# Experts' further tokens in a routed MoE: the loop's work rearranged, and x times its norm gathered in place of the modulated x

## The chip, the cores and the metric

The kernel runs on one core of one Trainium2 chip. The metric is the device time of one execution in microseconds (us). Before: 2464.49 us, the median of 3 runs (2462.65 to 2467.65).

## What is computed

A network with one sequence of 256 tokens, width 1024, in fp32: first two layers that each have an attention mixer and a routed mixture of experts (MoE), then two layers of another block. The change touches the two MoE alone. With `x` the residual stream:

```python
h = rmsnorm(x, norm_ffn[layer]) * (1.0 + scale_f) + shift_f
x = x + gate_f * grouped_moe(h, ...)

# grouped_moe: 16 experts in 4 groups, 2 experts of one group a token
aff = sigmoid(xf @ router_w)
biased = (aff + router_b).reshape(T, N_GROUPS, EXPERTS_PER_GROUP)
grp_score = sum(top_k(biased, 2)[0], axis=-1)
g_sel = argmax(grp_score, axis=-1)
local = top_k(biased[tok, g_sel], 2)[1]
w = aff[tok, expert] / sum(aff[tok, expert])
# every token of every one of its two experts
hid = silu(xb @ w_gate[e]) * (xb @ w_up[e])
out[token] += w * (hid @ w_down[e])
```

How many tokens an expert gets is known only when the kernel runs. The weights of a layer's experts are 96 MB, read once.

## The kernel before

A scheduler orders the instructions of the whole program for each engine by priority and dependence; the code's order is its starting point. Weights come by SyncE's (SP's) queue into a ring of 12 slots of 1 MB, "w" (`SLOTS`, `CAP`, L861); `load` (L890) takes the next slot and issues the transfer, `fill` (L928) asks for as many tiles ahead as `cap` allows, `take` hands them out in order. fp32 matmuls leave two records each in the trace; those of fp32r operands (a rounded high part and its rest, "h" and "l") leave one.

`router_prep` (L1104) runs ahead of a MoE, beside the mixer: it transposes `mod[4]`, which holds scale times gain, and `mod[3]`, the shift, and multiplies the router's weights with them.

`moe_body` (L1895), once a layer:
- transposes x, multiplies it with the router's weights, and makes `rs`, the inverse norm of each token (L1916). On DVE: logits z (L1927), sigmoid on ACT (L1928), the biased bz (L1931), the choice of group and experts in some 15 small operations, up to `selb` (L1957); on PE the position of each token within its expert; on DVE `OH` (L1976), a one-hot of expert slots, 64 a expert.
- for each of two halves of 128 tokens: h = x rs mod[4] on DVE (L1984), + mod[3] on POOL (L1985), its rounded part `hTh` on ACT (L1988) and the rest `hTl` on DVE (L1989). The last two read h with a step of 8 elements and write contiguously, so that a block of 128 columns is a contiguous stationary operand.
- `gather(b)`, four times, four experts each: 32 matmuls (L2020) with a 128x128 block of hTh or hTl stationary and 256 columns of OH moving give `xT`, the experts' tokens by columns; ACT copies it out of PSUM, 128x256 at a time (L2024).
- eight pairs q of experts: `gateup(q)` takes 8 tiles (L2048), silu and product follow, `down(q)` takes 4 tiles (L2066), `combine` scatters with the transposed one-hot and adds to x (L2086, L2088), one pair late.
- an expert's tokens beyond 64 go through `overflow` (L2126), called at q = 5 (`QL`). It is a loop whose number of passes is read at run time, one for each further 64 tokens of an expert: none in layer 0 of this input, one in layer 1.

A pass finds the expert on DVE (L2173 to L2178), reads its number into SP (L2179), and issues six transfers into six slots `lw` (L2183, L2186): gate and up, two tiles each, and down, two. The down product of a pass is `tail()` (L2150 to L2166): it is called within a pass for the pass before, and once behind the loop for the last one. Where there is no pass before, it multiplies zeros: POOL clears `hk`, `wk`, `ohT` and two whole `lw` tiles first (L2136). Between, the pass gathers its tokens (L2205 to L2218) and does gate and up (L2225 to L2231). Ahead of the loop `fill` asks for six tiles of q = 5 (`CAPL`).

```python
n = nc.values_load(nw[0:1, 0:1], min_val=0, max_val=7)
with s.tc.For_i(0, n, 1):
    ...
    ei = nc.sync.value_load(nw[0:1, 1:2], min_val=0, max_val=15)
    ...
    tail()
```

Of the kernel before, what the change touches and what calls it, by code (L numbers as in the profile page):

```python
# [57 lines left out]
class Kern:  # L58
# [781 lines left out]
class Full(Kern):  # L840
# [20 lines left out]
    SLOTS, CAP, SPL, DEEP, CAPL = 12, 11, 3, 7, 6  # L861
# [87 lines left out]
    def setup1(s):  # L949
# [15 lines left out]
        s.rlb = B1.tile([128, 16], F32, name="rlb")  # L965
        s.onesb = B1.tile([128, 128], BF, name="onesb")
# [3 lines left out]
        s.late.append(lambda: nc.sync.dma_start(s.rwp, I["router_w"].rearrange("(k p) e -> p k e", p=128)))  # L970
# [134 lines left out]
    def router_prep(s):  # L1105

        nc, V = s.nc, s.nc.vector
        for j in range(2):
            p = s.trans4(s.mod[4][:, j * 512:(j + 1) * 512])
            V.tensor_tensor(s.rwg[:, 4 * j:4 * j + 4, 0:16], s.rwp[:, 4 * j:4 * j + 4], p[:, :, 0:16], op=OP.mult)  # L1110
            yield
        q = s.bank("bg", (128, 16))
        for j in range(2):
            p = s.trans4(s.mod[3][:, j * 512:(j + 1) * 512])
            sh = s.a2("sh")
            nc.scalar.copy(sh, p)
            for k in range(4):
# [757 lines left out]
    def moe_srcs(s, l):  # L1875
        g, u, d = (s.I[n][l] for n in ("moe_w_gate", "moe_w_up", "moe_w_down"))
        out = []
        for m, j in s.FILL[l]:
            out += s.ada_src(m, j)
        for e in range(0, 16, 2):  # L1880
            for w in (g, u):
                for h in range(2):
                    for i in range(2):
                        out.append((w[e + i].rearrange("(p k) n -> p k n", p=128)[:, 4 * h:4 * h + 4], True))
            for h in range(2):
                for i in range(2):
                    out.append((d[e + i].rearrange("(p k) n -> p k n", p=128)[:, 2 * h:2 * h + 2], True))
        return out
# [6 lines left out]
    def moe_body(s, l, end):  # L1895
# [26 lines left out]
        nc.scalar.copy(lg, p)  # L1922
        p = s.bank("bg", (128, 2, 16))
# [33 lines left out]
        V.tensor_copy(selb, sel)  # L1957
# [20 lines left out]

        hh = []
        for t in range(2):  # L1980
            h = hb[t]
            hi = s.hp.tile([128, D], F32R, name=f"hTh{t}")
            lo = s.hp.tile([128, D], F32R, name=f"hTl{t}")
# [6 lines left out]
            hh.append((hi, lo))  # L1990
# [20 lines left out]
        def gather(b):  # L2011
            for i in range(2):
                xT[2 * b + i] = A.tile([128, 8, 128], F32, name="xT", tag="xT", bufs=3)
            for c in range(0, 8, 2):
                p = s.bg()
                for cc in range(2):
                    first = True
                    for t in range(2):
                        for x in hh[t]:
                            nc.tensor.matmul(p[:, cc * 256:(cc + 1) * 256], x[:, (c + cc) * 128:(c + cc + 1) * 128], OH[t][:, 4 * b:4 * b + 4],  # L2020
                                             start=first, stop=t == 1 and x is hh[t][1])
# [70 lines left out]
        for q in range(8):  # L2092
            if q == s.QL - 1:
                s.cap = s.CAPL
            if q == s.QL:
# [3 lines left out]
                tail = s.overflow(l, hh, pos, W, nx, cum)  # L2099
# [14 lines left out]
            if q == s.QL:  # L2114
                tail()
# [10 lines left out]
    def overflow(s, l, hh, pos, W, nx, cum):  # L2126

        nc, I, V, G, A = s.nc, s.I, s.nc.vector, s.nc.gpsimd, s.A
# [5 lines left out]
        lw = [s.wtile([128, 4, 512], name="lw") for i in range(6)]  # L2134
        for i, w in enumerate(lw):
            s.chain(G.memset(w if i > 3 else w[0:1, 0, 0:1], 0.0).ins)  # L2136
        wg = lw[:4]
        wd = [w.rearrange("p k n -> p (k n)").rearrange("p (k n) -> p k n", k=2) for w in lw[4:]]

        hk, wk, ohT = f("hk", 4, 64), f("wk", 1), A.tile([128, 256], F32R, name="ohT")  # L2140
        for x in (hk, wk):
            G.memset(x, 0.0)
        G.tensor_copy(ohT, hk.rearrange("p k s -> p (k s)"))

        def tail():
            p = s.mm()
            for h in range(2):
                for k in range(2):
                    for i in range(2):
                        nc.tensor.matmul(p[64 * i:64 * i + 64], hk[:, 2 * h + k], wd[h][:, k, i * 512:(i + 1) * 512],  # L2150
                                         start=h + k == 0, stop=h + k == 2)
            yf = s.a2("yf", (128, 512))
            for i in range(2):
                r = slice(64 * i, 64 * i + 64)
                V.scalar_tensor_tensor(yf[r], p[r], wk[r], s.mod[5][r, i * 512:(i + 1) * 512], op0=OP.mult, op1=OP.mult)
            yh, yl = (A.tile([128, 512], F32R, name=nm, bufs=2) for nm in ("yh", "yl"))
            nc.scalar.copy(yh, yf)
            V.tensor_tensor(yl, yf, yh.bitcast(F32), op=OP.subtract)
            for t in range(2):
                for i in range(2):  # L2160
                    r = slice(64 * i, 64 * i + 64)
                    p = s.bank("m2" if i else "bg")
                    for j, x in enumerate((yh, yl)):
                        nc.tensor.matmul(p, ohT[r, t * 128:(t + 1) * 128], x[r], start=j == 0, stop=j == 1)
                    xs = s.x[t][:, i * 512:(i + 1) * 512]
                    V.tensor_tensor(xs, p, xs, op=OP.add)  # L2166

        nw = A.tile([1, 2], I32, name="nw")
        V.tensor_copy(nw[:, 0:1], cum[0:1, 15:16])
        n = nc.values_load(nw[0:1, 0:1], min_val=0, max_val=7)  # L2170
        with s.tc.For_i(0, n, 1):  # L2171
# [7 lines left out]
            ei = nc.sync.value_load(nw[0:1, 1:2], min_val=0, max_val=15)  # L2179
            e = bass.ds(ei, 1)  # L2180
            for h in range(2):
                for i, w in enumerate(("moe_w_gate", "moe_w_up")):
                    nc.sync.dma_start(*s.flat(wg[2 * h + i], I[w][l][e].rearrange("o (p k) n -> p (o k) n", p=128)[:, 4 * h:4 * h + 4]))  # L2183
            tail()
            for h in range(2):
                nc.sync.dma_start(*s.flat(wd[h], I["moe_w_down"][l][e].rearrange("o (p k) n -> p (o k) n", p=128)[:, 2 * h:2 * h + 2]))  # L2186
# [15 lines left out]
            ohf = oh.rearrange("p t u s -> p t (u s)")  # L2202
            p = s.bank("tp", (128, 8))
# [3 lines left out]
            p = s.bg().rearrange("p (c s) -> p c s", c=8)  # L2207
            for c in range(8):
                first = True
                for t in range(2):  # L2210
                    for x in hh[t]:
                        nc.tensor.matmul(p[:, c], x[:, c * 128:(c + 1) * 128], oh[:, t, 0], start=first, stop=t == 1 and x is hh[t][1])
                        first = False
            xk = s.a2("xk", (128, 8, 64))
            nc.scalar.copy(xk, p)
# [50 lines left out]
```

## Time and profile before

| what | value |
|---|---|
| median of 3 runs | 2464.49 us (2462.65 to 2467.65) |
| the profiled execution, its own time | 2464.17 us |
| its span | 2462.4 us, 32028 instructions |
| PE busy | 2310.5 us (94%) |
| DVE, ACT, POOL busy | 1297.5, 1031.8, 411.6 us |
| DMA | 551.33 MB, mean 224 GB/s |
| MoE of layer 0 and 1, first gather to last product | about 253 to 506 us and 646 to 928 us |

The span is the profiled execution from its first to its last instruction; 1.8 us of the time lie around it. A share over the whole span mixes stages with different limits, so the rows below are of the MoE stretches alone. PE stands for the matmuls, PEld for the loads of the stationary operand; POOL is GpSimd. "<-" names what ended an idle time.

### The profile page before, as it was taken

What the parts mean: (1) busy time and instruction counts of PE and PEld (TensorE: products, weight loads), DVE (VectorE), ACT (ScalarE), POOL (GpSimd) and SP (SyncE); (2) the same over time, 40 slices, a digit from 0 to 9 for tenths busy, and PEclk for the clock granted to TensorE, in tenths of its full rate; (3) what the DMA queues carried; (4) which work ended last, traced back from release to release, by engine and by line L of the source; (5) the groups of instructions that cost most, each with busy time, mean ns of one, the idle gap of its engine ahead of it and who ended that gap; (6) DMA issues with size and microseconds to landing.
All of it is one profiled execution on the core that took longest, in us unless ns stands there. A gap on an engine that the chain in (4) does not pass through costs nothing.

```text
span 2462.4 us, 32028 instructions
## 1 busy us (share of the span) xinstructions
PE 2310.5 (94%) x12635; PEld 1636.8 (66%) x12635; DVE 1297.5 (53%) x2047; ACT 1031.8 (42%) x1615; POOL 411.6 (17%) x356
## 2 busy tenths in 40 slices
PE   6999999989899898999888999999999997999999
PEld 4755433356443436888777788887887776788887
DVE  4455222255422226555777756555555877765554
ACT  3454111044211105445655564444444754564543
POOL 1001000010100002002468510000001439620000
PEclk8999999989999898999999999999999998999999
DMA  9677798966799795555333355654655442445552
GB/s 346 242 262 255 320 420 365 415 231 232 290 419 382 300 383 189 188 190 198 132 139 121 138 168 170 204 187 163 205 188 195 167 142 90 135 159 196 172 188 69
DMA packets 241657, 551.33 MB, mean 224 GB/s; under 512 B 12639, under 2 KB 113864, under 8 KB 216160
## 3 DMA queue, kind: packets, MB, share of 16 engines
q1 hardware_dynamic: 241504, 549.26, 61.9%
q8 instruction: 100, 1.64, 0.3%
q14 instruction: 53, 0.43, 0.1%
HBM read 548.15 MB, written 1.06 MB: 223 GB/s over the span
## 4 chain that ended last, share of the span: by engine, by line
PE 62%; DVE 8%; POOL 5%; issue 2%; ACT 2%; DVEq 0%; ACTq 0%; POOLq 0%
PE mm L135 10%; PE mm L137 10%; PE mm L136 10%; PE mm L2048 5%; PE m L135 4%; PE m L136 4%; PE m L137 4%; DVE lo L917 3%; PE m L2066 2%; PE tp L187 2%; PE bg L136 2%; PE bg L135 2%; PE bg L137 2%; POOL rb L597 1%; PE bg L2020 1%
## 5 line engine op out<-in xcount | busy, mean ns | idle before, releaser
L917 DVE TENSOR_TENSOR lo<-w,hi 128x1024 fp32r<-128x1024 f32 (+1 forms) x520 | 659.5, 1308 | 422.0 <-issue 117.7
L915 ACT CAST hi<-w 128x1024 fp32r<-128x1024 f32 (+1 forms) x524 | 519.6, 1040 | 464.5 <-DVE lo L917 352.6
L135 PE MATMUL mm<-hi,hTh 128*128 128x512 f32 (+2 forms) x1200 | 482.4, 404 | 16.4 <-DVE rx L594 8.7
L136 PE MATMUL mm<-lo,hTh 128*128 128x512 f32 (+2 forms) x1200 | 473.4, 395 | 1.0 <-DVE lo L917 1.0
L137 PE MATMUL mm<-hi,hTl 128*128 128x512 f32 (+2 forms) x1200 | 471.9, 394 | 2.1 <-DVE hTl L192 1.8
L135 PEld LDWEIGHTS mm<-hi,hTh 128*128 128x128 f32 x1200 | 228.9, 191 | 65.4 <-DVE rx L594 10.2
L137 PEld LDWEIGHTS mm<-hi,hTl 128*128 128x128 f32 x1200 | 228.8, 191 | 53.3 <-DVE hTl L192 4.2
L2048 PE MATMUL mm<-w,xT 128*64 128x512 f32 x1024 | 259.4, 600 | 2.9 <-DVEq L2171 1.6
L136 PEld LDWEIGHTS mm<-lo,hTh 128*128 128x128 f32 x1200 | 229.7, 192 | 45.1 <-DVE lo L917 1.8
L2048 PEld LDWEIGHTS mm<-w,xT 128*64 128x64 f32 x1024 | 80.8, 137 | 141.4 <-issue 136.5
L135 PE MATMUL m<-hi,hTh 128*128 128x512 f32 x384 | 156.0, 407 | 9.2 <-DVE rx L594 8.9
L137 PE MATMUL m<-hi,hTl 128*128 128x512 f32 x384 | 153.4, 399 | 0.6 <-DVE hTl L192 0.6
L136 PE MATMUL m<-lo,hTh 128*128 128x512 f32 x384 | 153.7, 400 | 0.0
L2066 PE MATMUL m<-w,hidT 128*64 128x512 f32 x512 | 123.7, 597 | 7.7 <-ACT hidT L2059 6.6
L2053 DVE TENSOR_TENSOR sl<-mm,sl 128x512 f32<-128x512 f32 x16 | 11.1, 691 | 160.9 <-PE mm L2048 116.4
L135 PEld LDWEIGHTS m<-hi,hTh 128*128 128x128 f32 x384 | 73.9, 193 | 26.8 <-DVE rx L594 10.2
L2066 PEld LDWEIGHTS m<-w,hidT 128*64 128x64 f32 x512 | 41.1, 136 | 72.8 <-issue 61.5
L2071 DVE SCALAR_TENSOR_TENSOR yf<-m,wsl,mod 128x512 f32<-128x512 f32 x32 | 24.0, 750 | 114.9 <-PE m L2066 113.2
L137 PEld LDWEIGHTS m<-hi,hTl 128*128 128x128 f32 x384 | 73.6, 192 | 16.2 <-DVE hTl L192 1.0
L136 PEld LDWEIGHTS m<-lo,hTh 128*128 128x128 f32 x384 | 73.9, 192 | 15.3 <-DVE lo L917 0.8
L204 POOL TENSOR_TENSOR rs<-ss,mhalf 128x1 f32<-128x1 f32 x18 | 11.0, 611 | 427.1 <-DVE ss L202 427.0
L191 ACT CAST hidh<-tp 128x256 fp32r<-128x256 f32 x88 | 32.3, 372 | 101.2 <-PE tp L187 101.1
(610 smaller groups left out, 3492.5 us busy)
## 6 DMA issues: line engine op xcount, KB each, us to landing
w<-in_ffn_w_in_dram SPq DMA_DIRECT2D x176, 512.0 KB, 4.9
w<-in_w_in_dram SPq DMA_DIRECT2D x84, 1024.0 KB, 4.9
w<-in_moe_w_gate_dram SPq DMA_DIRECT2D x64, 1024.0 KB, 10.8
w<-in_moe_w_up_dram SPq DMA_DIRECT2D x64, 1024.0 KB, 13.9
w<-in_moe_w_down_dram SPq DMA_DIRECT2D x64, 1024.0 KB, 12.3
w<-in_ada_w_dram SPq DMA_DIRECT2D x48, 1024.0 KB, 7.4
w<-in_ffn_w_out_dram SPq DMA_DIRECT2D x44, 1024.0 KB, 4.9
w<-in_ev_w_in_dram SPq DMA_DIRECT2D x10, 1024.0 KB, 6.6
```

The source lines that it names most:

```text
L135: nc.tensor.matmul(out, xh, wh, start=first, stop=False)
L136: nc.tensor.matmul(out, xh, wl, start=False, stop=False)
L137: nc.tensor.matmul(out, xl, wh, start=False, stop=last)
L187: s.nc.tensor.transpose(p[:, i], src[:, i * 128:(i + 1) * 128], s.ident)
L191: s.nc.scalar.copy(hi, p)
L597: G.tensor_tensor(b[:, :, o:o + 64], x[:, :, i:i + 64], sn[:, t, None, o:o + 64].to_broadcast([128, 4, 64]), op=OP.mult)
L915: a = s.nc.scalar.copy(hi[:, h], t[:, h]).ins
L917: b = eng.tensor_tensor(lo[:, h], t[:, h], hi[:, h].bitcast(F32), op=OP.subtract).ins
L2020: nc.tensor.matmul(p[:, cc * 256:(cc + 1) * 256], x[:, (c + cc) * 128:(c + cc + 1) * 128], OH[t][:, 4 * b:4 * b + 4], start=first, stop=t ...
L2048: nc.tensor.matmul(p[64 * i:64 * i + 64], xT[q][:, 4 * h + k, 64 * i:64 * i + 64], ws[i][:, k], start=h + k == 0, stop=h + k == 4)
L2066: nc.tensor.matmul(ps[n][64 * i:64 * i + 64], hT[:, 2 * h + k, 64 * i:64 * i + 64], ws[i][:, k, n * 512:(n + 1) * 512], start=h + k == 0, ...
L2071: V.scalar_tensor_tensor(yf, ps[n], wsl[:, q:q + 1], s.mod[5][:, n * 512:(n + 1) * 512], op0=OP.mult, op1=OP.mult)
```

## The change

- hTh and hTl are now made of x rs alone (ACT's L1940, a copy with a scale for each token; DVE's L1942), contiguously, ahead of the sigmoid. The product with mod[4] and the sum with mod[3] are made when xT is taken out of PSUM, by 16 pieces of 128x128 a gather, half on ACT (L2040) and half on DVE (L2038); `mT`, their columns, come from `router_prep`.
- The stationary operands of the gather, and of the transposes of x and of the modulation, are now read with a step of 4 fp32 elements.
- The gate and up tiles are contiguous blocks of 512 rows.
- `overflow` prepares the first pass's expert, tokens and weights at q = 2 (`window`, `weights`); `loop()` at q = 5 has four `lw` slots; a pass does gate and up, then its own down product out of the first two slots, and prepares the next pass between. Nothing follows the loop. `CAPL` is 5.

```diff
+    def transp(s, src, j):
+        p = s.bank("tp", (128, 4, 128))
+        v = src[:, j * 512:(j + 1) * 512].rearrange("t (p k) -> t k p", k=4)
+        for k in range(4):
+            s.nc.tensor.transpose(p[:, k], v[:, k], s.ident)
...
-    SLOTS, CAP, SPL, DEEP, CAPL = 12, 11, 3, 7, 6
+    SLOTS, CAP, SPL, DEEP, CAPL = 12, 11, 3, 7, 5
...
-                        out.append((w[e + i].rearrange("(p k) n -> p k n", p=128)[:, 4 * h:4 * h + 4], True))
+                        out.append((w[e + i, 512 * h:512 * h + 512].rearrange("(p k) n -> p k n", p=128), True))
...
+        hh = []
+        for t in range(2):
+            hi = s.hp.tile([128, D], F32R, name=f"hTh{t}")
+            lo = s.hp.tile([128, D], F32R, name=f"hTl{t}")
+            nc.scalar.activation(hi, s.x[t], AF.Copy, scale=rs[:, t:t + 1])
+            hh.append((hi, lo))
+        lows = lambda t: V.scalar_tensor_tensor(hh[t][1], s.x[t], rs[:, t:t + 1], hh[t][0].bitcast(F32), op0=OP.mult, op1=OP.subtract)
+        lows(0)
...
-        V.tensor_copy(selb, sel)
+        q = V.tensor_copy(selb, sel).ins
+        s.after(lows(1).ins, q.name)
+        hv = [[x.rearrange("t (h p k) -> t h k p", h=2, k=4) for x in y] for y in hh]
...
-            V.scalar_tensor_tensor(h, s.x[t], rs[:, t:t + 1], s.mod[4], op0=OP.mult, op1=OP.mult)
-            G.tensor_tensor(h, h, s.mod[3], op=OP.add)
-
-            hv, hiv, lov = h.rearrange("t (p k) -> t k p", k=8), *(x.rearrange("t (k p) -> t k p", k=8) for x in (hi, lo))
-            nc.scalar.copy(hiv, hv)
-            V.tensor_tensor(lov, hv, hiv.bitcast(F32), op=OP.subtract)
...
-                            nc.tensor.matmul(p[:, cc * 256:(cc + 1) * 256], x[:, (c + cc) * 128:(c + cc + 1) * 128], OH[t][:, 4 * b:4 * b + 4],
+                            nc.tensor.matmul(p[:, cc * 256:(cc + 1) * 256], x[:, (c + cc) // 4, (c + cc) % 4], OH[t][:, 4 * b:4 * b + 4],
...
-                for i in range(2):
-                    nc.scalar.copy(xT[2 * b + i][:, c:c + 2], p.rearrange("p (c i s) -> p c i s", c=2, i=2)[:, :, i])
+                for cc in range(2):
+                    m = s.mT[:, c + cc:c + cc + 1], s.mT[:, 8 + c + cc:9 + c + cc]
+                    for i in range(2):
+                        o, x = xT[2 * b + i][:, c + cc], p[:, cc * 256 + i * 128:cc * 256 + i * 128 + 128]
+                        if i:
+                            V.tensor_scalar(o, x, m[0], m[1], op0=OP.mult, op1=OP.add)
+                        else:
+                            nc.scalar.activation(o, x, AF.Identity, bias=m[1], scale=m[0])
...
-                tail = s.overflow(l, hh, pos, W, nx, cum)
+                loop()
...
-            if q == s.QL:
-                tail()
+            if q == 2:
+                loop = s.overflow(l, hh, pos, W, nx, cum)
...
+        weights(*window())
+
+        def loop():
+            lw = [s.wtile([128, 4, 512], name="lw") for i in range(4)]
...
+            with s.tc.For_i(0, n, 1):
+                ei = nc.sync.value_load(nw[0:1, 1:2], min_val=0, max_val=15)
...
+                nxt = window()
+                p = s.mm()
+                for h in range(2):
+                    for k in range(2):
+                        for i in range(2):
+                            nc.tensor.matmul(p[64 * i:64 * i + 64], hk[:, 2 * h + k], wd[h][:, k, i * 512:(i + 1) * 512],
...
+                weights(*nxt)
```

`window()` gathers 64 tokens with the one-hot stationary and x times its norm moving, 8 matmuls of 128x512 (L2187), transposes the result (4) and scales it to `xk` (L2193); `weights()` makes `wk` and `ohT` with two matmuls and two transposes (L2200, L2204). The scratch for dynamic DMAs is 1024 bytes, and the router's weights are loaded in longer runs.

How the order moves, in layer 0, at three places.

DVE at the start of the MoE, from the norm to the routing (z: logits, bz: biased affinities, adat: a part of the next layer's conditioning). Before:

```order
L1984 SCALAR_TENSOR_TENSOR h<-x_70,rs_1942,mod_1496 128x1024
L1984 SCALAR_TENSOR_TENSOR h<-x_71,rs_1942,mod_1496 128x1024
L1927 SCALAR_TENSOR_TENSOR z<-bg,rs_1942,rlb 128x16 x2
L1098 SCALAR_TENSOR_TENSOR adat<-abias,ident,bg 128x512
L1931 TENSOR_TENSOR bz<-aff,rb 128x32
L1936 TENSOR_TENSOR s_1992<-bz 128x8x2 x2
L1936 TENSOR_TENSOR s_1992<-bz 128x8 x2
L1948 TENSOR_TENSOR gt<-bz 128x128
```

After:

```order
L1948 SCALAR_TENSOR_TENSOR z<-bg,rs_1947,rlb 128x16 x2
L1942 SCALAR_TENSOR_TENSOR hTl_1990<-x_70,rs_1947,hTh_1989 128x1024
L1952 TENSOR_TENSOR bz<-aff,rb 128x32
L1107 SCALAR_TENSOR_TENSOR adat<-abias,ident,bg 128x512
L1957 TENSOR_TENSOR s_2004<-bz 128x8x2 x2
L1957 TENSOR_TENSOR s_2004<-bz 128x8 x2
```

The two products h are gone, the first rest stands in their place behind z, and bz comes ahead of adat.

SP ahead of the loop and in it (w: the ring's tiles, lw: those of a pass, nw: the expert's number). Before:

```order
L901 DMA w<-in_moe_w_gate_dram 128x2048 x4
L901 DMA w<-in_moe_w_up_dram 128x2048 x2
L2171 COMPARE_AND_BRANCH
L2171 UNCONDITIONAL_BRANCH x2
L2261 BRANCH_PREFETCH_HINT
L2179 TENSOR_LOAD nw
L2179 ISA x2
L2183 ISA
L2183 DMA lw<-in_moe_w_gate_dram 128x2048
```

After:

```order
L909 DMA w<-in_moe_w_gate_dram 128x2048 x4
L909 DMA w<-in_moe_w_up_dram 128x2048 x4
L2215 COMPARE_AND_BRANCH
L2215 UNCONDITIONAL_BRANCH x2
L2288 BRANCH_PREFETCH_HINT
L2216 TENSOR_LOAD nw
L2216 ISA x2
L2220 ISA
L2220 DMA lw<-in_moe_w_gate_dram 128x2048
```

Eight tiles of the next pair instead of six are asked for ahead of the loop; within it the same six transfers follow, of which the two down weights now go into the first two slots of gate and up.

PE in a pass. Before, the beginning of it, with the product for the pass before in front (L2150, L2164; the gather L2212 and gate and up L2225 follow further down):

```order
L2150 MATMUL mm<-lw,hk 64x512 x8
L2205 MATMUL tp<-wt,ohk 128x1
L2218 MATMUL tp<-ident,ohk 128x128
L2205 MATMUL tp<-wt,ohk 128x1
L2218 MATMUL tp<-ident,ohk 128x128
L2164 MATMUL bg<-yh,ohT 128x512
L2164 MATMUL m_2947<-yh,ohT 128x512
L2164 MATMUL bg<-yh,ohT 128x512
```

After:

```order
L2226 MATMUL mm<-lw,xk 64x512 x16
L187 MATMUL tp<-ident,gu 128x128 x4
L2241 MATMUL mm<-lw,hk 64x512 x4
L2187 MATMUL bg<-hTh_1989,ohk 128x512
L2187 MATMUL bg<-hTl_1990,ohk 128x512
L2187 MATMUL bg<-hTh_1989,ohk 128x512
L2187 MATMUL bg<-hTl_1990,ohk 128x512
L2187 MATMUL bg<-hTh_1992,ohk 128x512
L2187 MATMUL bg<-hTl_1993,ohk 128x512
L2187 MATMUL bg<-hTh_1992,ohk 128x512
L2187 MATMUL bg<-hTl_1993,ohk 128x512
L2241 MATMUL mm<-lw,hk 64x512 x4
```

Gate and up (L2226) come first, the pass's own down product (L2241) follows, the gather of the next pass (L2187) stands between its halves, and the product in front is gone, as is the one behind the loop.

## Rows read from the trace of the kernel before

**Rows 1.** Windows: stretch, length, busy us (instructions) per engine, PEclk, DMA share, GB/s.

```profile
300.00:330.00 30.00, 30.00 (x156) 14.56 (x156) 9.04 (x15) 4.56 (x10) 0.00 (x0) 1.00 1.01 419
402.00:409.00 7.00, 3.93 (x16) 1.54 (x14) 5.28 (x8) 1.24 (x2) 3.56 (x2) 1.00 0.09 35
795.00:805.00 10.00, 8.50 (x30) 3.10 (x28) 7.34 (x22) 1.24 (x2) 3.56 (x2) 0.83 0.03 12
805.00:821.00 16.00, 12.84 (x60) 9.24 (x58) 5.32 (x10) 1.58 (x3) 0.00 (x0) 0.68 0.95 381
821.00:832.00 11.00, 8.94 (x34) 2.77 (x32) 0.42 (x1) 0.97 (x2) 0.00 (x0) 0.81 0.04 18
```

**Rows 2.** PE's waits in layer 1's MoE: us in total, times, longest; the largest.

```profile
PE tp L187 <- DVE sl L2053: 4.2, 5, 0.9
```

**Rows 3.** Timeline, start of layer 0's MoE: start, us, engine, line, out<-in, [idle before <-releaser].

```profile
236.90 2.48 DVE L1984 SCALAR_TENSOR_TENSOR h<-x,rs,mod 128x1024 f32<-128x1024 f32 x2 [0.88 <-POOL rs L1916]
...
238.27 5.66 POOL L1985 TENSOR_TENSOR h<-h,mod 128x1024 f32<-128x1024 f32 x2 [1.40 <-DVE h L1984]
...
241.64 2.10 ACT L1988 CAST hTh<-h 128x1024 fp32r<-128x1024 f32 x1 [1.70 <-POOL h L1985]
...
241.97 2.00 DVE L1931 TENSOR_TENSOR bz<-aff,rb 128x32 f32<-128x32 f32 x1
...
243.16 1.92 PE L1095 MATMUL bg<-w,cl 128*32 128x512 f32 x16
...
245.75 1.98 DVE L1989 TENSOR_TENSOR hTl<-h,hTh 128x1024 fp32r<-128x1024 f32 x1
...
247.92 0.74 DVE L1098 SCALAR_TENSOR_TENSOR adat<-abias,ident,bg 128x512 f32<-128x512 f32 x1
...
251.85 0.18 DVE L1957 CAST selb<-sel 128x32 bf16<-128x32 f32 x1
...
253.16 0.55 PE L2020 MATMUL bg<-OH,hTh 128*128 128x256 f32 x1 [0.80 <-DVE OH L1976]
```

**Rows 4.** Timeline, start of layer 1's MoE.

```profile
636.41 1.92 PE L1095 MATMUL bg<-w,cl 128*32 128x512 f32 x16
...
646.48 0.55 PE L2020 MATMUL bg<-OH,hTh 128*128 128x256 f32 x1 [0.79 <-DVE OH L1976]
```

**Rows 5.** Timeline: successive matmuls of a gather, and in layer 1's loop.

```profile
260.74 0.28 PE L2020 MATMUL bg<-OH,hTh 128*128 128x256 f32 x1
...
260.86 0.29 PE L2020 MATMUL bg<-OH,hTl 128*128 128x256 f32 x1
...
811.33 0.40 PE L2212 MATMUL bg<-ohk,hTh 128*128 128x64 f32 x1
...
811.54 0.40 PE L2212 MATMUL bg<-ohk,hTl 128*128 128x64 f32 x1
```

**Rows 6.** ACT, strided rounding (min/median/max ns) and the page's contiguous cast (busy us, mean ns).

```profile
L1988 ACT CAST hTh<-h x4: 2032/2090/2147, 241.6 to 639.0; 128x1024 fp32r<-128x1024 f32 x4
...
L915 ACT CAST hi<-w 128x1024 fp32r<-128x1024 f32 (+1 forms) x524 | 519.6, 1040 | 464.5 <-DVE lo L917 352.6
```

**Rows 7.** Timeline, loop place of layer 1.

```profile
797.13 3.56 POOL L2136 MEMSET lw<- 128x2048 f32 x2 [3.25 <-PE m L2066]
...
801.81 4.62 PE L2150 MATMUL mm<-lw,hk 128*64 128x512 f32 x16
...
804.82 0.37 SPq L2183 DMA_DIRECT2D lw<-in_moe_w_gate_dram  x1
...
818.60 9.89 PE L2225 MATMUL mm<-lw,xk 128*64 128x512 f32 x32 [0.68 <-ACT xk L2215]
...
831.21 3.99 PE L2048 MATMUL mm<-w,xT 128*64 128x512 f32 x10 [1.32 <-DVE hk L2231]
```

**Rows 8.** Timeline, loop place of layer 0.

```profile
403.05 3.56 POOL L2136 MEMSET lw<- 128x2048 f32 x2 [3.25 <-PE m L2066]
...
408.81 3.65 PE L2048 MATMUL mm<-w,xT 128*64 128x512 f32 x16 [1.56 <-DVEq L2171]
```

More of the change, by code (lines that the diff above doesn't have):

```diff
@@ L965, in setup1 @@
         s.rlb = B1.tile([128, 16], F32, name="rlb")
+        s.mT = B1.tile([128, 16], F32, name="mT")
         s.onesb = B1.tile([128, 128], BF, name="onesb")
@@ L1113, in router_prep @@
         for j in range(2):
-            p = s.trans4(s.mod[3][:, j * 512:(j + 1) * 512])
+            p = s.transp(s.mod[3], j)
             sh = s.a2("sh")
             nc.scalar.copy(sh, p)
+            V.tensor_copy(s.mT[:, 8 + 4 * j:12 + 4 * j], sh[:, :, 0])
             for k in range(4):
@@ L2018, in gather @@
                     for t in range(2):
-                        for x in hh[t]:
-                            nc.tensor.matmul(p[:, cc * 256:(cc + 1) * 256], x[:, (c + cc) * 128:(c + cc + 1) * 128], OH[t][:, 4 * b:4 * b + 4],
-                                             start=first, stop=t == 1 and x is hh[t][1])
+                        for x in hv[t]:
+                            nc.tensor.matmul(p[:, cc * 256:(cc + 1) * 256], x[:, (c + cc) // 4, (c + cc) % 4], OH[t][:, 4 * b:4 * b + 4],
+                                             start=first, stop=t == 1 and x is hv[t][1])
                             first = False
-                for i in range(2):
-                    nc.scalar.copy(xT[2 * b + i][:, c:c + 2], p.rearrange("p (c i s) -> p c i s", c=2, i=2)[:, :, i])
+                for cc in range(2):
[6 more added lines that the diff above has]
+                            nc.scalar.activation(o, x, AF.Identity, bias=m[1], scale=m[0])
         def transOH(q):
@@ L2133, in overflow, with window @@
         G.memset(kf, 0.0)
[L2134 to L2166, printed above, removed]
+        xk, wk, ohT = f("xk", 8, 64), f("wk", 1), A.tile([128, 256], F32R, name="ohT")
         nw = A.tile([1, 2], I32, name="nw")
         V.tensor_copy(nw[:, 0:1], cum[0:1, 15:16])
-        n = nc.values_load(nw[0:1, 0:1], min_val=0, max_val=7)
-        with s.tc.For_i(0, n, 1):
+        def window():
             ind, tmp, r = f("ind", 16), f("tmp", 2, 16), f("r", 4)
@@ L2202, in overflow, with weights @@
             ohf = oh.rearrange("p t u s -> p t (u s)")
+            xg = s.a2("xg", (128, 512))
+            for i in range(2):
+                p = s.bg()
+                first = True
+                for t in range(2):
+                    for x in hh[t]:
+                        nc.tensor.matmul(p, ohf[:, t], x[:, 512 * i:512 * i + 512], start=first, stop=t == 1 and x is hh[t][1])
+                        first = False
+                r = slice(64 * i, 64 * i + 64)
+                nc.scalar.copy(xg[r].rearrange("t (k p) -> t k p", k=4), p[r].rearrange("t (p k) -> t k p", k=4))
+            p = s.trans4(xg)
+            for i in range(2):
+                V.tensor_tensor(xk[:, 4 * i:4 * i + 4], p[:, :, 64 * i:64 * i + 64], s.mT[:, 4 * i:4 * i + 4, None].to_broadcast([128, 4, 64]), op=OP.mult)
+            V.tensor_tensor(xk, xk, s.mT[:, 8:16, None].to_broadcast([128, 8, 64]), op=OP.add)
+            return ohf, wt
+        def weights(ohf, wt):
             p = s.bank("tp", (128, 8))
@@ L2206, in overflow @@
             V.tensor_copy(wk, p[:, 0:1])
[L2207 to L2215, printed above, removed]
             p = s.bank("tp", (128, 2, 128))
@@ L2235 @@
+        return loop
 _INS = ["x", "c", "rel_table", "router_w", "router_b", "final_norm", "norm_mix", "norm_ffn", "ada_w", "ada_b",
```

73 lines of the change are left out of this document (44 added, 29 removed).

## The prediction

> **What bounds the kernel now.** I read the windows of the MoE stretches first, then the list of what TensorE (PE) waits for, then the timeline at the three places that the diff touches: the start of a layer's MoE, the gathers, and the loop over further tokens. In a window inside the eight expert pairs PE is busy 30.00 of 30.00 us at a granted clock of 1.00, and the DMA engines are at 1.01 with 419 GB/s [rows 1]: both are full, PE by its matmuls, the DMAs because the weight slots free just as fast as they are refilled. The list of PE's waits in layer 1 decides which of the two is first: its largest entry is a round trip over DVE of at most 0.9 us at a time [rows 2], and none of its entries names a weight transfer. So inside MoE what comes off PE's chain comes off the time, and a transfer that starts earlier buys nothing by itself. Three places are different, since PE is not full there: the loop place in layer 0 (3.93 us busy in 402 to 409), the loop place in layer 1 (three windows from 795 to 832, clock 0.83, 0.68 and 0.81, DMA share 0.03, 0.95, 0.04) [rows 1], and the start of a layer, where the first gather waits for DVE.
>
> **Start of a layer.** In layer 0 DVE makes x times norm times scale (2.48 us for both halves), POOL adds the shift (5.66), ACT rounds each half with a strided read (2.10), DVE forms each rest (1.98), and in between the routing runs on DVE in small steps; the routing step bz takes 2.00 us because it stands until POOL's long add is over; selb starts at 251.85 and the first gather matmul at 253.16 [rows 3]. The change takes off DVE 2.48 + 2 x 1.98, and about 1.8 of bz (its neighbours of the same size, such as selb, take 0.18). It puts back two rests from contiguous operands, 1.28 each by the multiply that it removes, which reads and writes as much: 8.24 - 2.56 = 5.7 us less on DVE. Not all of that reaches the gather. ACT's two roundings now stand ahead of the sigmoid's table load, 2 x 1.04 [rows 6] where nothing stood, which moves the sigmoid to about 240.7; and DVE then meets the conditioning's second half, whose PE matmuls end at 243.16 + 1.92 = 245.08 [rows 3] and are not moved. From there on DVE runs in a row: adat 0.74, selb 0.18, the second rest 1.28, a mod row 0.7 (as long as adat), and W, pos, counts and the first one-hots, which take 1.1 now from selb's end to the gather: 4.0 [rows 3]. That is 245.1 + 4.0 = 249.1 in place of 253.16: **-4.0 us**. In layer 1 the same matmuls end at 638.33 and the gather starts at 646.48 [rows 4]; the mod row is ACT's there (0.7 less), so 638.4 + 3.6 = 642.0: **-4.5 us**. If the two halves of the removed work were already hidden, the least that remains is bz's standing, 1.8 us a layer; more than 5.7 a layer isn't to be had. The next weight loads are tied to the first gate/up tile and move with it.
>
> **Evictions of the gather.** Sixteen 128x128 pieces in place of eight 128x256. ACT keeps eight, each at most what one is now, so no more work than before; DVE gets eight, between selb's 0.18 for 128x32 and adat's 0.74 for 128x512 [rows 3]: 1.4 to 6 us a gather, beside PE work of which DVE uses 9.04 in 30 us [rows 1]. I cost it at nothing; uncovered, in the first gather, it would be some 1 us, since the two engines share the pieces.
>
> **The loop place in layer 0 (no pass).** Removed from PE is the product that always ran after the loop: 16 matmul records at 3.65 / 16 = 0.23 us [rows 8] and 8 of half height, at most the same: 5.5, and I take 5.2. Put on PE, at pair 2, is the window made ahead: 8 of 128x512 at 0.23 = 1.8, and 12 small ones at 0.12 [rows 5] = 1.4; together 3.2. PE is full there, so both count whole. The removed clearing of two whole weight slots on POOL, 403.05 to 406.61, ended 2.2 us before PE goes on at 408.81 [rows 8], beside the last additions of pair 4, and was covered by them. Eight weight tiles instead of six are now asked for before the loop, the last two when their slots come free, at 403 as that clearing shows; 2 MB at 419 GB/s are 5 us, with 1 or 2 of latency 409 to 410, where the engines leave the loop now: 0 to 1.2 us, 0.6 taken. **-1.4 us**.
>
> **The loop place in layer 1 (one pass).** Before, from the end of pair 4's down product, when POOL gets its last slots (797.13), to PE's next gate/up (831.21) is 34.1 us, and the product afterwards is 5.2: 39.3. The first load of the pass goes out at 804.82, behind DVE's search for the expert; PE does an empty product meanwhile (4.62) and the pass's gate/up in 9.89, half of it at a lower clock [rows 7]. After: the expert is known since pair 2, so the four loads leave at once, but behind two further tiles that use the last slots, freed at 797.1 [rows 7]. 1 MB takes 2.5 us at 419 GB/s: the two tiles end at 802.4, the first two of the pass at 807.4, the last two at 812.4; with 1.5 us of latency 809 and 814. Gate/up of the first half is 16 such records, 3.7 us, or 6.8 at half the clock; the down weights can only then be asked for, into the same slots, and land 5 us and a latency after the fourth load, 820 to 821.5. Rounding, transposes, silu and product, each as now, end about then too. Down product 3.7 to 4.6, next window 1.8, two scalings and a rest at adat's 0.74 [rows 3] and a rounding at half of 1.04 [rows 6], 2.7; scatter, 8 matmuls of half height, 1.2; four additions 2.8: PE is free at 833 to 836.7. From 797.1 that is 37.7 in the middle, and 3.2 for the window ahead: 40.9, **+1.6 us** (-2 to +4).
>
> **The strided weights of PE.** Now a 128-column stationary operand of the gather is contiguous; afterwards its elements lie four fp32 (16 bytes) apart. This holds for 128 loads a layer, and for 16 transposes of x and 16 of the modulation. No PE operand before is strided so, and the price must be bounded. Below: none, if reading isn't what paces the load. Above: ACT's rounding with a strided read took 2.09 us, its contiguous cast of the same size 1.04 [rows 6], a factor of 2, at a stride of 32 bytes, though. When only 64 columns follow, a load and its matmul go out every 0.21 us at half the clock [rows 5], so 0.107 at full clock is what a contiguous load needs; doubled, 0.215 against the gather's pitch of 0.12 [rows 5]: +0.095 x 256 = 24 us, and some 5 for the transposes. I take none: at full clock the gather's 256 moving columns go through in 0.12 us, four fp32 in 1.9 ns, while a stationary column has 0.84 ns at present, and the only rows of a slow read are of other engines and of twice the stride. This is the choice on which the sign rests, and it is not a safe one.
>
> [...]
>
> **Sum.** -4.0 - 4.5 - 1.4 + 1.6 = -8.3 us. The profiled execution took 2464.17 (span 2462.4), 0.3 under the median of 2464.49; so 2456 against the median. The first layers' contiguous 1 MB blocks (the rows of a half are taken in one piece), the router weights' layout and the smaller scratch change no term: transfers run at 419 GB/s already and PE doesn't wait for them.
>
> **Rivals.**
> *A, the strided loads cost.* Mechanism as above: the stationary load becomes longer than the 0.12 us of its matmul. It decides from a pitch of 0.15 us, where 0.03 x 256 eat the 8 us. At a factor 1.5 a load is 0.16: +10 and 3 for the transposes, 2469; at 2, +24 and 5, 2485; I take 2480. For it speaks ACT's doubling at a stride; against it, that the stride is half as long, and that a stationary column has twice the time of a moving one.
> *B, the pass gets no shorter and the lead is given back.* PE stands from 802 to 809 for the pass's weights with nothing to do, where it now runs an empty product, and the windows show the clock at 0.68 after such a stretch [rows 1]; the gate/up at half the clock throughout, then the down weights 3 later, an exit that waits for the additions: layer 1's loop is +5 rather than +1.6. With DMA at 1.01 everywhere an earlier start of PE by 4 us may also use up the lead of the 12 slots, and the weights, not PE, then set the later pairs: half of the 8.5 us returns. 2464.5 - 8.3 + 3.4 + 4 = 2463.6. For it: the DMA share; against it: PE's list has no wait for a weight.
> *C, the gain of the start is larger than the chain that I built* (5.7 in each layer), and the window ahead hides in PE's waits: 2452. Part of the forecast's own range, 2451 to 2461.
>
> **Chances.** Forecast with C 0.43, A 0.37, B 0.20. A difference under 0.2%, 5 us, can't be told from none here, so faster begins under 2459.5. Of the forecast's 0.43 some 0.03 lies above that, B gives 0.03 below it: faster 0.43. B and the forecast's rest: same 0.19; of A 0.01 lies there as well. Slower: nearly all of A and 0.02 of B, 0.38. The range 2451 to 2485 leaves out a fifth of A and the ends of the others.
>
> **What would show it.** The pitch of the gather's matmuls at full clock: 0.12 keeps the forecast, 0.15 ends it, 0.2 is A. First gather about 4 us sooner than 253.16, and 4.5 sooner than 646.48, counted from each layer's router. PE's next gate/up behind the loop of layer 1 36 to 40 us after the last down product of pair 4, no empty product after it, and windows there with a DMA share that has no gap of 8 us before the pass. B would show as weight transfers in PE's list of waits or a clock under 0.7 over the whole pass. The prediction is wrong if the strided loads cost over 0.03 us each, or if PE's chain at the start waits for something that isn't in it now.

## The result, and the profile after

The changed kernel takes 2496.7 us (median of 4 runs, 2494.33 to 2497.67), the kernel before 2464.83 (4 runs beside it): a ratio of 1.0127, interval 1.011 to 1.0145. It is 32 us slower, outside the range. The profiled executions show 30.0 of it: spans of 2492.4 and 2462.4.

The first thing to read is the gather, in the timeline of the changed kernel at half clock and then at full (start, us, engine, line):

```profile
248.60 0.44 PE L2030 MATMUL bg<-OH,hTh 128*128 128x256 f32 x1
248.84 0.43 PE L2030 MATMUL bg<-OH,hTl 128*128 128x256 f32 x1
249.07 0.43 PE L2030 MATMUL bg<-OH,hTh 128*128 128x256 f32 x1
...
258.77 0.40 PE L2030 MATMUL bg<-OH,hTl 128*128 128x256 f32 x1
259.00 0.40 PE L2030 MATMUL bg<-OH,hTh 128*128 128x256 f32 x1
259.23 0.40 PE L2030 MATMUL bg<-OH,hTl 128*128 128x256 f32 x1
```

From one matmul to the next it is 0.23 us at either clock. Before, it was 0.12 at full clock [rows 5] and 0.21 at half, as the last two rows here show. The windows are of the change at 248.2 and 258, and of the kernel before at 253.1 (columns as in [rows 1]); the two matmuls are of the kernel before:

```profile
248.20:249.40 1.20, 1.20 (x7) 1.20 (x7) 0.94 (x6) 0.46 (x1) 0.00 (x0) 0.50 0.95 373
258.00:260.00 2.00, 2.00 (x10) 2.00 (x9) 0.00 (x0) 0.00 (x0) 0.00 (x0) 1.00 0.83 270
253.10:254.40 1.30, 1.24 (x6) 1.27 (x7) 1.30 (x6) 0.00 (x0) 0.00 (x0) 0.50 0.38 95
...
253.51 0.41 PE L2020 MATMUL bg<-OH,hTl 128*128 128x256 f32 x1
253.72 0.41 PE L2020 MATMUL bg<-OH,hTh 128*128 128x256 f32 x1
```

So the price is one of full clock: at half clock a contiguous operand is nearly as slow. The groups of the gather's line, min/median/max ns, show which half of the work it is, before (L2020) and in the change (L2030):

```profile
L2020 PEld LDWEIGHTS bg<-OH,hTh x128: 186/189/331, 253.1 to 850.1; 128*128 128x128 f32 x128
...
L2030 PEld LDWEIGHTS bg<-OH,hTh x128: 307/329/335, 245.5 to 876.9; 128*128 128x128 f32 x128
...
L2030 PE MATMUL bg<-OH,hTh x128: 390/396/609, 245.5 to 877.0; 128*128 128x256 f32 x128
```

The load of 128 columns takes 329 ns at the median; before it is 189. A matmul of 256 columns goes out only every 0.23 us, in step with the longer load; e3_stairs below changes the step of the load alone.

The start of layer 0's MoE, timeline of the changed kernel, to hold against [rows 3]:

```profile
233.00 0.71 POOL L1927 TENSOR_TENSOR rs<-ss,mhalf 128x2 f32<-128x2 f32 x1 [40.13 <-DMA w<-in_moe_w_up_dram]
...
240.07 1.92 PE L1104 MATMUL bg<-w,cl 128*32 128x512 f32 x16
...
242.06 0.75 DVE L1107 SCALAR_TENSOR_TENSOR adat<-abias,ident,bg 128x512 f32<-128x512 f32 x1 [0.21 <-PE bg L1104]
...
242.72 0.17 DVE L1978 CAST selb<-sel 128x32 bf16<-128x32 f32 x1
...
242.81 1.28 DVE L1942 SCALAR_TENSOR_TENSOR hTl<-x,rs,hTh 128x1024 fp32r<-128x1024 f32 x1
...
245.54 0.48 PE L2030 MATMUL bg<-OH,hTh 128*128 128x256 f32 x1 [1.44 <-DVE OH L1999]
```

POOL's norm ends at 233.71 and the gather begins 11.8 us later; before, DVE's first product waited for the norm till 236.90 and the gather came 16.3 us after that [rows 3]. DVE's second adat (242.06) and the rest behind selb stand as they were built up in the prediction.

The loop places, windows of the changed kernel (columns as in [rows 1]) and timeline:

```profile
402.00:416.00 14.00, 9.88 (x40) 3.79 (x36) 5.38 (x8) 1.24 (x2) 0.09 (x1) 0.86 0.62 228
820.00:840.00 20.00, 12.21 (x38) 4.11 (x39) 5.92 (x21) 0.64 (x2) 0.00 (x0) 0.74 0.88 349
840.00:857.00 17.00, 11.23 (x52) 5.15 (x51) 6.89 (x14) 3.12 (x6) 0.00 (x0) 0.86 0.20 83
```

```profile
405.26 4.19 SPq L909 DMA_DIRECT2D w<-in_moe_w_up_dram  x3
...
413.42 0.69 DVE L2104 TENSOR_TENSOR x<-bg,x 128x512 f32<-128x512 f32 x1 [0.19 <-PE bg L2102]
...
416.68 2.03 SPq L909 DMA_DIRECT2D w<-in_moe_w_down_dram  x4
...
417.14 6.19 PE L2064 MATMUL mm<-w,xT 128*64 128x512 f32 x16 [3.77 <-issue]
```

In layer 0 nothing runs in the loop, and yet PE's first gate/up behind it waits 3.77 us for no engine that the profile names ("issue"). SP asked for the last three tiles from 405.26 on, goes on at 416.68, and the loop is left only then; SP's own list of waits says 5.5 us for these transfers. The 16 records then take 6.19 us in place of 3.65 [rows 8]; the clock is 0.50 from 412.5 on, before the wait begins, and still at 420. In layer 1, in the pass:

```profile
821.66 0.36 SPq L2220 DMA_DIRECT2D lw<-in_moe_w_gate_dram  x1
...
829.95 1.94 PE L2226 MATMUL mm<-lw,xk 128*64 128x512 f32 x2 [6.35 <-DMA lw<-in_moe_w_gate_dram]
...
836.67 1.17 SPq L2228 DMA_DIRECT2D lw<-in_moe_w_down_dram  x2
...
843.36 1.94 PE L2241 MATMUL mm<-lw,hk 128*64 128x512 f32 x8 [1.00 <-DVE hk L2235]
...
856.72 6.13 PE L2064 MATMUL mm<-w,xT 128*64 128x512 f32 x14 [2.53 <-DVE x L2257]
```

The pass's loads go out at 821.66, behind those tiles, and PE waits 6.35 us for the first. SP asks for the down weights when the first half of gate and up is done (836.67), and PE goes on with the next pair at 856.72, behind the additions.

To see what each stretch lost I took the 16 copies of a pair's hidden rows on ACT (L2059, later L2075 and others) from each timeline as marks, and the starts of the norm on POOL and of the first gather. Us between marks:

| stretch | before | change | step 2 (e9b) | step 2, six slots (e9) | loop alone (e5) | loop alone, six slots (e6) |
|---|---|---|---|---|---|---|
| layer 0: norm to first gather | 17.00 | 12.54 | 12.01 | 12.03 | 16.79 | 17.02 |
| first gather to pair 0 | 28.64 | 33.71 | 27.51 | 27.51 | 28.58 | 28.63 |
| pair 0 to 1 | 22.41 | 24.44 | 22.60 | 22.60 | 22.42 | 22.42 |
| pair 1 to 3 (with the window ahead) | 60.58 | 66.73 | 63.60 | 63.61 | 62.48 | 62.47 |
| pair 3 to 4 | 30.48 | 30.49 | 30.49 | 30.50 | 30.49 | 30.49 |
| pair 4 to 5 (loop place) | 40.03 | 47.18 | 43.92 | 38.38 | 41.40 | 38.71 |
| pair 5 to 7 | 58.09 | 57.47 | 57.47 | 57.47 | 60.92 | 60.92 |
| layer 1: norm to first gather | 15.49 | 11.54 | 11.41 | 11.74 | 15.52 | 15.51 |
| first gather to pair 0 | 28.57 | 31.60 | 26.25 | 26.26 | 28.78 | 28.53 |
| pair 0 to 1 | 23.72 | 25.24 | 23.40 | 23.40 | 23.72 | 23.72 |
| pair 1 to 3 | 60.10 | 68.68 | 65.13 | 65.13 | 62.61 | 62.61 |
| pair 3 to 4 | 30.48 | 30.49 | 30.49 | 30.49 | 30.49 | 30.48 |
| pair 4 to 5 (loop place) | 69.96 | 74.51 | 69.68 | 60.38 | 70.40 | 59.63 |
| pair 5 to 7 | 58.25 | 61.29 | 61.30 | 61.31 | 55.97 | 55.97 |

The change's column is 32.1 us over before's. The norm of layer 0 came 3.2 us sooner in this profile. That isn't credited to an edit: e3_stairs is the same program up to layer 1, and there the norm starts where it did before (236.15 against 236.16). The four right columns are from the experiments.

### The profile page after: what moved, and what is told of

Its sections match the earlier page's. It is cut to its first block, busy times and chain, and to the rows that moved or that the text cites. A ratio compares the mean times of both kernels' runs of the same rounds, so it can differ in the third digit from the quotient of the medians.

```text
span 2492.4 us, 32056 instructions
## 1 busy us (share of the span) xinstructions
PE 2338.1 (94%) x12603; PEld 1657.9 (67%) x12603; DVE 1306.6 (52%) x2144; ACT 1037.2 (42%) x1620; POOL 395.2 (16%) x342
## 4 chain that ended last, share of the span: by engine, by line
PE 50%; DVE 7%; POOL 6%; issue 1%; ACT 1%; DVEq 0%; POOLq 0%; ACTq 0%
PE mm L135 9%; PE mm L137 9%; PE mm L136 9%; PE m L135 4%; PE m L136 4%; PE m L137 4%; DVE lo L925 3%; PE mm L2064 2%; PE tp L187 2%; PE bg L135 2%; PE bg L136 2%; PE bg L137 1%; POOL rb L605 1%; PE m L2082 1%; POOL ra L603 1%
## 5 line engine op out<-in xcount | busy, mean ns | idle before, releaser
L2082 PE MATMUL m<-w,hidT 128*64 128x512 f32 x512 | 130.0, 597 | 6.4 <-ACT hidT L2075 6.2
L137 PEld LDWEIGHTS m<-hi,hTl 128*128 128x128 f32 x384 | 73.7, 192 | 16.3 <-DVE hTl L200 1.0
L2040 ACT ACTIVATE xT<-bg,mT 128x128 f32<-128x128 f32 x64 | 28.8, 457 | 125.5 <-PE bg L2030 114.2
L2104 DVE TENSOR_TENSOR x<-bg,x 128x512 f32<-128x512 f32 x64 | 42.0, 686 | 67.9 <-PE bg L2102 67.9
```

Of the source, the lines that this page charges most:

```text
L137: nc.tensor.matmul(out, xl, wh, start=False, stop=last)
L2040: nc.scalar.activation(o, x, AF.Identity, bias=m[1], scale=m[0])
L2082: nc.tensor.matmul(ps[n][64 * i:64 * i + 64], hT[:, 2 * h + k, 64 * i:64 * i + 64], ws[i][:, k, n * 512:(n + 1) * 512], start=h + k == 0, ...
```

## Experiments

**e1_contig: a contiguous stationary operand.** Theory S: the strided loads. Rival L: the loop places.

```diff
-            nc.scalar.activation(hi, s.x[t], AF.Copy, scale=rs[:, t:t + 1])
+            nc.scalar.activation(kp(hi), pk(s.x[t]), AF.Copy, scale=rs[:, t:t + 1])
```

(kp and pk are views of "t (h k p)" and "t (h p k)" with the axes k p; the rest likewise, in two halves.) 

> The changed kernel, but the rounding on ACT and the rests on DVE read x with the step of 4 elements and write contiguous blocks of 128 columns, so that the gather's stationary operand is contiguous again; everything else as in the change. Theory S (the strided stationary loads are what costs: pitch of the gather at full clock 0.233 us in place of 0.118 over 256 matmuls, some 27 us): pitch back to 0.12, and 2496.7 - 27 + 2 to 4 for the strided rounding at the start of each layer = 2472 (2467 to 2476). Rival L (most of the loss is at the loop places, by exits and by what waits behind them): above 2485.

2466.24 us, ratio to before 1.0007 (0.9998 to 1.0017): 30 us back, a little under the range of theory S, and rival L falls. The rounding pays in turn: 2164 ns on ACT for a read with a step of 16 bytes, against 1148 in the change (medians of the groups, 4 each).

**e3_stairs: four steps in one kernel.**

```diff
-        hv = [[x.rearrange("t (h p k) -> t h k p", h=2, k=4) for x in y] for y in hh]
+        hs = [[[x.rearrange("t (h p k) -> t h k p", k=st, p=128) for x in y] for y in hh] for st in (1, 2, 4, 8)]
...
+            st = (0, 1, 3, 0)[b] if l else 2
+            hv, st = hs[st], 1 << st
```

In layer 1 only which columns of the hidden rows lie in a block of the gather differs.

> The changed kernel, but in layer 1 the four gathers read their stationary blocks with steps of 1, 2, 8 and 1 elements (4, 8, 32 and 4 bytes) in place of 4 (16 bytes); the columns of the experts' tokens are then in another order there, so that layer 1's experts see permuted inputs. [...] If the price grows with the distance: between 0.118 and 0.233 at step 2, well above 0.233 at step 8.

One execution, 2484.61 us. The groups of the gather's line in e3_stairs, in the windows of layer 1 in which each step ran (1: 658 to 668, 2: 670 to 700, 8: 730 to 752):

```profile
L2032 PEld LDWEIGHTS bg<-OH,hTh x16: 186/188/192, 658.1 to 667.8; 128*128 128x128 f32 x16
L2032 PEld LDWEIGHTS bg<-OH,hTh x12: 193/195/198, 677.9 to 687.2; 128*128 128x128 f32 x12
L2032 PEld LDWEIGHTS bg<-OH,hTh x16: 313/338/341, 734.6 to 748.1; 128*128 128x128 f32 x16
```

188, 195 and 338 ns at 4, 8 and 32 bytes, and 329 at 16 in the change: a cliff between 8 and 16 bytes, and little more beyond it; no step between those two was run. The timeline of the same kernel shows the pitch, at step 2 and at step 8:

```profile
687.25 0.28 PE L2032 MATMUL bg<-OH,hTl 128*128 128x256 f32 x1
687.36 0.28 PE L2032 MATMUL bg<-OH,hTh 128*128 128x256 f32 x1
687.49 0.28 PE L2032 MATMUL bg<-OH,hTl 128*128 128x256 f32 x1
...
747.96 0.40 PE L2032 MATMUL bg<-OH,hTl 128*128 128x256 f32 x1
748.19 0.41 PE L2032 MATMUL bg<-OH,hTh 128*128 128x256 f32 x1
748.44 0.41 PE L2032 MATMUL bg<-OH,hTl 128*128 128x256 f32 x1
```

687.25 to 687.49 is two matmuls at step 2, 0.12 each; 747.96 to 748.44 two at step 8, 0.24 each. The price isn't one of distance: from 8 to 16 bytes the load grows by 134 ns, from 16 to 32 by 9. What makes the cliff no run shows.

**e9b_step2: the change with a step of 2.** The cleanest undoing: what changes is which columns lie in a block, and with them the rows of the weights (the shown line is one of several).

```diff
-        hv = [[x.rearrange("t (h p k) -> t h k p", h=2, k=4) for x in y] for y in hh]
+        hv = [[x.rearrange("t (h p k) -> t h k p", h=4, k=2) for x in y] for y in hh]
```

> The change with one thing altered: the step of every stationary operand is 2 elements (8 bytes) in place of 4; the rows of the gate, up and router weights are taken in the order that fits (a tile in pieces of 4 KB), hi and lo parts stay contiguous and the start as quick as in the change, loop as in the change. [...] If e1_contig gained by something else than the stride of the stationary operand (its rounding, its order of instructions): above 2480.

2468.1 us, ratio to before 1.0012 (1.0003 to 1.0021): 28.6 us less than the change, and not above 2480. e1_contig's 2466.24 less its slower rounding, 4 x (2164 - 1148) ns = 4.1 us, would be 2462, an estimate; this is 6 above it. Its loads:

```profile
L2030 PEld LDWEIGHTS bg<-OH,hTh x128: 193/195/201, 249.6 to 851.3; 128*128 128x128 f32 x128
```

By the table its stretches are shorter by 15.0 us in layer 0 and 15.7 in layer 1, of which 256 loads x 0.114 are 29. The stretches without a gather (3 to 4, 5 to 7) stay as in the change. What is left against before (3.8 us, while the start alone is 9 shorter) must be elsewhere.

**e5_loop: the loop alone, on the kernel before.** Its `overflow` is the change's, with the gather's operands as they were.

```diff
-    SLOTS, CAP, SPL, DEEP, CAPL = 12, 11, 3, 7, 6
+    SLOTS, CAP, SPL, DEEP, CAPL = 12, 11, 3, 7, 5
...
-                tail = s.overflow(l, hh, pos, W, nx, cum)
+                loop()
...
-            if q == s.QL:
-                tail()
+            if q == 2:
+                loop = s.overflow(l, hh, pos, W, nx, cum)
```

> The kernel before with the loop of the change alone (prepared at pair 2, own down product, four slots, eight tiles ahead); start, gather and evictions as before, no strided stationary operand. If the loop place costs what the milestones of the two traces leave for it when the strided loads are taken out (about +6 in layer 0, +4 in layer 1): 2475 (2470 to 2479). If the loop's work is neutral and the losses there came only from strided loads nearby: 2465 within 3. As predicted for the loop: the same, 2465.

2471.15 us, ratio 1.0026 (1.0014 to 1.0037). Slower without any strided operand: the loop isn't neutral. I had it at 0 (-1.4 + 1.6); it is +7.

**e2_six and e6_loop_six: six slots,** the first on e1_contig, the second on e5_loop.

```diff
-    SLOTS, CAP, SPL, DEEP, CAPL = 12, 11, 3, 7, 5
+    SLOTS, CAP, SPL, DEEP, CAPL = 12, 11, 3, 7, 6
...
-            lw = [s.wtile([128, 4, 512], name="lw") for i in range(4)]
+            lw = [s.wtile([128, 4, 512], name="lw") for i in range(6)]
...
-            wd = [w.rearrange("p k n -> p (k n)").rearrange("p (k n) -> p k n", k=2) for w in lw[:2]]
+            wd = [w.rearrange("p k n -> p (k n)").rearrange("p (k n) -> p k n", k=2) for w in lw[4:]]
```

> As e1_contig, and the loop has six weight slots again, with the down weights in slots of their own, and six tiles of the next pair ahead of it instead of eight. Theory S and a second cost at the loop (in layer 0 its exit waits for the two tiles asked for last, 4 to 5 us and a fall of the clock behind it; in layer 1 the pass's loads stand behind those tiles, PE waits 6.4 us for them): both waits go, 2472 - 14 = 2458 (2454 to 2463). Rival: the pass is bound by PE's own chain and the exit by the additions on DVE, then the same as e1_contig within 3 us.

> As e5_loop (the kernel before with the loop of the change alone), with six weight slots, the down weights in slots of their own and six tiles ahead. If the exit and the pass lose what e2_six lost against e1_contig (10.4 us): 2461 (2458 to 2464), a little under the kernel before. If that gain came from the start or the gathers: 2471 as e5_loop.

2455.86 (ratio 0.9965, 0.9951 to 0.9979) and 2456.26 (0.9965, 0.9952 to 0.9978): 10.4 us under e1_contig and 14.9 under e5_loop, more than was expected of the second (2458 to 2464). PE's wait at the exit in layer 0 falls from 4.00 to 1.57 and from 4.37 to 1.52, that for the pass's first weights from 6.3 to 2.1 in two parts, and from 6.5 to none that the list names. The loop of the change by itself is worth 8 us against before if it has its slots. The edit moves the slots, the place of the down weights and the number of tiles ahead together; no run separates them. In layer 0, where no pass runs, it can only be the tiles ahead.

The half clock behind the exit does not go away with the wait. First gate/up behind the loop of layer 0, timeline of e2_six (first row) and e6_loop_six (second):

```profile
410.01 5.35 PE L2067 MATMUL mm<-w,xT 128*64 128x512 f32 x16 [1.57 <-DVEq L2218]
```

```profile
411.07 5.23 PE L2048 MATMUL mm<-w,xT 128*64 128x512 f32 x16 [1.52 <-DVEq L2198]
```

The kernel before waited as long (1.56) and had them in 3.65 [rows 8]. In e6_loop_six the windows show 0.50 from 407.5 on, ahead of the wait.

That both end at the same time is not explained by one stretch. e2_six's start, with its slower rounding, is only 1.2 us shorter than e6_loop_six's (16.57 and 14.79 us from the norm to the first gather), and the rest of the two kernels differs by a few us either way from stretch to stretch.

**e8_write: contiguous reads, writes with a step,** on e2_six.

```diff
-        pk = lambda x: x.rearrange("t (h p k) -> t h k p", h=2, k=4)
-        kp = lambda x: x.rearrange("t (h k p) -> t h k p", h=2, k=4)
+        pk = lambda x: x.rearrange("t (h p k) -> t h p k", h=2, k=4)
+        kp = lambda x: x.rearrange("t (h k p) -> t h p k", h=2, k=4)
```

> As e2_six, but the rounding and the rests read x contiguously and write with a step (128 elements) where e2_six read with a step of 4 elements and wrote contiguously. [...] If writes pay as much: no change, 2456.

2457.92 us, no gain. ACT's rounding is at 2090 ns (2164 with strided reads), DVE's halves at 1117 (1140): a write with a step pays as much as a read. ACT is the clean case, since DVE also reads hTh with that step here. Had only reads paid, ACT's rounding would be near the 1148 ns of the change; that falls.

**e7_router: the strided transposes and the router's weights in longer runs, on the kernel before** (two of its edits are shown).

```diff
-            p = s.trans4(s.mod[4][:, j * 512:(j + 1) * 512])
+            p = s.transp(s.mod[4], j)
...
-                p = s.trans4(s.x[t][:, j * 512:(j + 1) * 512])
+                p = s.transp(s.x[t], j)
```

> The kernel before with the router part of the change alone: the router's weights are loaded in runs of 256 bytes instead of 64, and x and the modulation are transposed with the step of 4; gathers, evictions and loop as before. In the trace of the change the first mixer is 1.5 us ahead at 60 us and 3.4 at 80, which the loop alone (e5_loop) didn't show. If that comes from the router's weights in a stretch where the DMAs are the bound: 3 us less, 1 given back by strided transposes, 2462 (2460 to 2464). If it was the start of the program that varies from run to run: 2464 to 2466.

2463.18 against 2464.7, ratio 0.9994 (0.9985 to 1.0003): no difference that can be told, though the time lies in the range of the first reading. Its norm of layer 0 starts 1.6 us later than before's, that of the change 3.2 sooner, e2_six's 0.5 sooner with the same edit, one profile of each: the start of the program varies by this much.

**e9_step2_six: step 2 and six slots together,** e9b_step2 with the edit of e2_six.

> As e9b_step2, with six weight slots in the loop, the down weights in slots of their own and six tiles ahead. If the loop's two waits are independent of the start: 10 less than e9b_step2, as e2_six against e1_contig: 2452 (2448 to 2457), which would be under both kernels. If a start that is 4 us sooner in each layer is given back later, because the weights then set the pace: 2456, as e2_six and e6_loop_six.

2454.16 us, ratio 0.9958 (0.9945 to 0.9972): faster than both kernels, 10 us under before. It lies half way between the two readings, 2452 and 2456, and only 2.1 us under e6_loop_six, whose start is 8.8 us longer by the table. Timeline of e9b_step2 (first row) and of e9_step2_six (second) behind the loop of layer 0, the first gate/up:

```profile
410.45 6.24 PE L2064 MATMUL mm<-w,xT 128*64 128x512 f32 x16 [4.61 <-issue]
```

```profile
406.15 3.65 PE L2064 MATMUL mm<-w,xT 128*64 128x512 f32 x16 [1.67 <-DVEq L2215]
```

The exit waits 1.67 us, for the last addition, in place of 4.61 for transfers. The 16 records take 3.65 us in place of 6.24; this profile is the only one of the six-slot kernels in which the clock holds there (5.35, 5.23 and 5.26 us in e2_six, e6_loop_six and e8_write). In the table the loop place is 5.5 us shorter in layer 0 and 9.3 in layer 1.

## Why the prediction was wrong

- **Start of a layer: right.** -4.0 and -4.5 forecast; -4.5 and -4.0 measured (17.00 to 12.54, 15.49 to 11.54), and by the same chain. That it is kept to the end isn't shown: the start of e9_step2_six is 5.0 and 3.8 us shorter than that of e6_loop_six, and it ends only 2.1 us sooner.
- **The strided weights: the step that failed.** "I take none." Of the 40 us between forecast and result this is 29, and the loop 7. The price is 0.114 us for each of 256 loads at full clock, 29 us, a little over the upper bound that I had built (24, a doubling of 0.107 us). My argument was that a stationary column has more time than a moving one. But the load takes 188 ns at a step of 4 bytes, 195 at 8 and 329 at 16, so the time that a column has did not cover the price. The strided rows of ACT and DVE were the better evidence, though of other engines: DVE's rest took 1.98 us strided [rows 3] and takes 1.28 contiguous, and ACT at 16 bytes (2164 ns) costs what it does at 32 (2090, [rows 6]), which no row of before could tell. Rival A was the mechanism, at 0.37, and a pitch over 0.15 was its sign. Its time of 2480 was 17 low: the load was 5 dearer and the loop 7; the rest, some 5, no run takes alone; it may lie in the order of the work (below). The 5 that I had for the transposes show in no run (e7_router).
- **The loop place in layer 0: sign wrong.** -1.4 forecast. In e5_loop, the loop without strided loads, it is +6. The window ahead is +1.9 (pair 1 to 3; 3.2 forecast). Pair 4 to 5 is +1.4: the wait at the exit is 4.4 us against 1.6 and the 16 records behind it 5.9 against 3.7, together +5.0, and the removed product gives back 3.7, not 5.2. I had costed the exit at 0.6, from a landing at 409 to 410; three tiles were asked for late, not two, and records at half the clock were not in the sum. The last 2.8 are in pairs 5 to 7, where the scheduler set PE's work in another order.
- **The loop place in layer 1: near.** +1.6 forecast; e5_loop has +2.5 for the window ahead (3.2 forecast), +0.4 at the loop and -2.3 in the last pairs, +0.7 in all. The order of the loads was read rightly (behind the tiles, PE waiting): in the change PE is back 37.3 us after the end of pair 4's down product (819.4 to 856.72), 37.7 forecast.
- **The order of the work elsewhere: in no term.** e9b_step2 is some 6 us above what a start 9 shorter and a loop 7 longer would give. The largest piece that the table shows is pairs 5 to 7 of layer 1, 61.30 us against 55.97 in e5_loop and 58.25 before. A down product there takes 9.1 us in place of 7.4, its records being set in another order, and PE waits 0.7 us for ACT behind it, where the scatter now follows at once. In layer 0 the last gather is cut into seven pieces between gate/up records, where e5_loop has four. The listing of the order would have shown this. No run takes it alone, so its share stays open.
- **Evictions: not at nothing.** ACT takes 457 ns for a 128x128 piece with scale and shift, longer than the 374 for a copy of 128x256; "each at most what one is now" was wrong. It stayed covered: in e9b_step2 PE's list of waits has 0.3 us for an xT.
- **Rival B** has no run for it. Its longer pass didn't come (+0.4 at the loop in e5_loop). A start that is mostly given back later did come, but no list names a wait for a weight outside the pass, so the weights aren't shown as its cause. That pair 3 to 4 is 30.48 to 30.50 in all six kernels of the table tells little, since e1_contig does it in 28.01 with its records in another order.

## What to carry to other kernels

Look at the innermost step of every operand that an edit turns over to another engine, the stationary one of a matmul too: here 8 bytes took the gather's load from 189 to 195 ns and 16 to 329, so a layout with half the step kept the shorter start. When slots are taken from a ring around a loop, follow what the freed slots are used for: transfers that were asked for ahead of it were waited for at its exit here, even where it made no pass. When a forecast gains in one stretch, list the order of the work behind it too: the new start gained 9 us, and some 6 were lost again in stretches that no term covered. And an upper bound built from rows of another engine is worth more chance than a reason why it shouldn't hold.

## What was not expected of the hardware

- The stationary load of 128 fp32r columns takes 188, 195, 329 and 338 ns at steps of 4, 8, 16 and 32 bytes; at 16 bytes its pitch is 0.23 us at full clock and at half, contiguous 0.12 and 0.21.
- ACT pays as much for a write with a step of 512 bytes as for a read with one of 16 (2090 and 2164 ns for 128x1024, 1148 contiguous on both sides).
- The time of the 16 matmul records behind the loop's exit doesn't follow from PE's wait there alone: waits of 3.7 to 4.6 us were followed by 5.9 to 6.2 us, but waits of 1.5 to 1.7 by 3.65 in three kernels (before, e7_router, e9_step2_six) and by 5.2 to 5.4 in three (e2_six, e6_loop_six, e8_write).
